# A softmax with temperature on one core: all transfers on one queue in a fixed order, in pieces of 6 MB, with the row maximum subtracted

## The chip, the cores and the metric

The kernel runs on one core of a Trainium2 chip. The metric is the device time of one execution in microseconds (us), lower is better.

## The reference

```python
x = randn(32, 512, 1024).astype(float32); temperature = 0.5
scaled = x / temperature
shifted = scaled - max(scaled, axis=-1, keepdims=True)
exp_x = exp(shifted)
return exp_x / sum(exp_x, axis=-1, keepdims=True)
```

That is 16,384 rows of 1,024 numbers: 67.1 MB read and 67.1 MB written, with about one exponential and one multiplication for each number. In both kernels these 134.2 MB pass through the DMA engines of the core.

## The kernel before

Four rows for each of 128 partitions make a tile of 2 MB. Loads are issued on SP, stores on ACT (two queues), and a pool of eight buffers with automatic waits keeps them running side by side. The kernel doesn't subtract the maximum; with this data (normal numbers times two) the exponential doesn't overflow.

```python
K_MAIN = 4
SPLIT_LAST = 4
# ... sched = 32 tiles of K = 4
data = ctx.enter_context(tc.tile_pool(name="data", bufs=8))
for it, (g0, K) in enumerate(sched):
    # ... xv, ov: rows (p k) of this tile, 16 KB in one piece per partition
    xtile = data.tile([P, K, d], mybir.dt.float32)
    nc.sync.dma_start(out=xtile.rearrange("p k d -> p (k d)"), in_=xv)          # L47
    for j in range(K):
        nc.scalar.activation(xtile[:, j, :], xtile[:, j, :], Exp,               # L52
                             scale=scale, accum_out=sums[:, j : j + 1])
    nc.vector.reciprocal(recip, sums)                                           # L59
    for j in range(K):
        nc.vector.tensor_scalar_mul(xtile[:, j, :], in0=xtile[:, j, :],         # L61
                                    scalar1=recip[:, j : j + 1])
    if it >= ntiles - SPLIT_LAST and K > 1:
        h = K // 2
        nc.scalar.dma_start(out=ov[:, :h, :], in_=xtile[:, :h, :])
        nc.sync.dma_start(out=ov[:, h:, :], in_=xtile[:, h:, :])
    else:
        nc.scalar.dma_start(out=ov, in_=xtile)                                  # L70
```

Of the kernel before, what the change touches and what calls it, by code (L numbers as in the profile page):

```python
# [1 line left out]

# [4 lines left out]


@with_exitstack  # L10
def kernel(
    ctx: ExitStack,
    tc: tile.TileContext,
    x: bass.AP,
    temperature: bass.AP,
    out: bass.AP,
):
    nc = tc.nc
    scale = 1.0 / float(temperature)

    P = 128
    xf = x.flatten_outer_dims()
    of = out.flatten_outer_dims()
    n, d = xf.shape
    nrowgroups = n // P

    K_MAIN = 4
    SPLIT_LAST = 4
    sched = []
    g = 0  # L30
    while g < nrowgroups:
        k = min(K_MAIN, nrowgroups - g)
        sched.append((g, k))
        g += k
    ntiles = len(sched)

    data = ctx.enter_context(tc.tile_pool(name="data", bufs=8))
    stats = ctx.enter_context(tc.tile_pool(name="stats", bufs=16))

    for it, (g0, K) in enumerate(sched):  # L40
        rows = P * K
        r0 = g0 * P
        xv = xf[r0 : r0 + rows, :].rearrange("(p k) d -> p (k d)", p=P, k=K)
        ov = of[r0 : r0 + rows, :].rearrange("(p k) d -> p k d", p=P, k=K)

        xtile = data.tile([P, K, d], mybir.dt.float32)
        nc.sync.dma_start(out=xtile.rearrange("p k d -> p (k d)"), in_=xv)  # L47

        sums = stats.tile([P, K], mybir.dt.float32)
        recip = stats.tile([P, K], mybir.dt.float32)  # L50
        for j in range(K):
            nc.scalar.activation(  # L52
                xtile[:, j, :],
                xtile[:, j, :],
                mybir.ActivationFunctionType.Exp,
                scale=scale,
                accum_out=sums[:, j : j + 1],
            )
        nc.vector.reciprocal(recip, sums)  # L59
        for j in range(K):  # L60
            nc.vector.tensor_scalar_mul(  # L61
                xtile[:, j, :], in0=xtile[:, j, :], scalar1=recip[:, j : j + 1]
            )

        if it >= ntiles - SPLIT_LAST and K > 1:
            h = K // 2
            nc.scalar.dma_start(out=ov[:, :h, :], in_=xtile[:, :h, :])  # L67
            nc.sync.dma_start(out=ov[:, h:, :], in_=xtile[:, h:, :])
        else:
            nc.scalar.dma_start(out=ov, in_=xtile)  # L70


# [1 line left out]
_INS = ['x', 'temperature']  # L74
_OUTS = [((32, 512, 1024), 'float32')]
#: Inputs that are plain numbers.
_NUMBERS = {'temperature': 0.5}


# [26 lines left out]
```

## Time and profile before

| | before |
|---|---|
| time, median | 319.7 us (319.55 to 319.85, 3 runs) |
| span of the profiled execution | 317.8 us |
| DVE / ACT busy | 29% / 43% |
| moved | 134.26 MB, 422 GB/s over the span |

The page's first two parts for the kernel before. The rows of 40 digits divide the span into slices of 7.9 us; a digit is the busy share in tenths, and 9 means 90% or more.

```profile
span 317.8 us, 636 instructions
...
DVE 93.4 (29%) x160; ACT 138.0 (43%) x257; POOL 0.2 (0%) x4
...
DVE  0352333312300517631333213333123003733300
ACT  1875334554321739655334553345543106852500
DMA  7999999999999999999999999999999999999996
GB/s 297 429 394 429 431 431 434 435 433 433 433 429 429 432 429 429 429 429 431 429 433 434 433 435 431 429 433 431 431 429 429 431 429 431 437 429 430 422 426 271
```

DVE and ACT are mostly idle. DMA is full in every slice but the first and the last, at about 430 GB/s. Below are the two queues (packets, MB, share of the 16 DMA engines' time) and the chain that ended last, by engine: the two queues share the same engines half and half, and 91% of the chain is DMA.

```profile
q1 hardware_dynamic: 5184, 71.31, 52.9%
q10 hardware_dynamic: 4608, 62.92, 46.3%
...
DMA 91%; ACT 1%; SPq 1%; DVE 1%; issue 0%; DVEq 0%; ACTq 0%
```

The costliest groups (busy us, mean ns of one, idle time before them), and the transfers (KB each, median us from issue to landing):

```profile
L52 ACT ACTIVATE xtile<-xtile 128x1024 f32<-128x1024 f32 x128 | 133.5, 1044 | 159.3 <-DMA xtile<-in_x_dram 158.2
L61 DVE TENSOR_SCALAR xtile<-xtile,recip 128x1024 f32<-128x1024 f32 x128 | 87.7, 749 | 1.1
...
xtile<-in_x_dram SPq DMA_DIRECT2D x32, 2048.0 KB, 31.3
out_dram<-xtile ACTq DMA_DIRECT2D x28, 2048.0 KB, 24.2
```

Every activation and every multiplication is short against the time that DMA takes for the tile: load and store of 2 MB each are 9.8 us of DMA, against 4 x 1.04 us of ACT and 4 x 0.75 us of DVE.

The last stretches of 2 us (start:end of the stretch, its length, busy time of DVE, ACT and POOL with counts, PEclk, DMA share, GB/s). A packet's bytes are booked where it starts, so a share can exceed 1 and the last rows run a little ahead of the true ends.

```profile
312.00:314.00 2.00, 0.00 (x0) 0.00 (x0) 0.00 (x0) 1.00 1.00 422
314.00:316.00 2.00, 0.00 (x0) 0.00 (x0) 0.00 (x0) 1.00 0.46 193
316.00:318.00 2.00, 0.00 (x0) 0.00 (x0) 0.00 (x0) 1.00 0.01 4
```

The DMA engines run out of work between 314 and 316 us, and the span closes at 317.8.

The page gives the mean of 16 DMA engines.

- *Ends of single engines.* The trace holds a record of each DMA packet (start, duration, size, queue). On a busy engine a packet starts within some 4 ns of the end of the one before, so the records fall into 16 chains, one per engine, by matching ends and starts. A few chains swap partners where two engines happen to run in step, so single chains are approximate; the 16 end times are not affected.
- *Lag of a transfer.* Each transfer is spread over the 16 engines, and each engine adds one completion write to the transfer's semaphore when its share has landed. (The Trainium skill says so in "DMA: Bandwidth & Descriptors", section "Why a DMA increments its semaphore by 16 and not by 1"; the trace agrees: 68 transfers here, and 1,088 packets under 512 B on the queues.)

### The profile page before, as it was taken

Reading aid. Unit: us, or ns where it says so; the run is one execution under the profiler, and the core shown is the slowest. Engines: PE = TensorE matmul, PEld = TensorE weight load, DVE = VectorE, ACT = ScalarE, POOL = GpSimd, SP = SyncE. Lnnn points to the kernel's source line nnn. Section 1 sums busy time; section 2 is a strip of 40 time slices with the busy share of each in tenths; the row PEclk is TensorE's granted clock in tenths of the full one; section 3 lists DMA queues with packets and bytes.
Section 4 is the critical chain, followed back from the end, with each engine's and each line's share of the span. In section 5 each row is a group of like instructions: output and inputs, shape, how many; then the busy total and the mean of one; then the engine's idle time right before and its main releaser. Section 6 shows DMA issues by size and latency. Waiting matters only on the chain.

```text
span 317.8 us, 636 instructions
## 1 busy us (share of the span) xinstructions
DVE 93.4 (29%) x160; ACT 138.0 (43%) x257; POOL 0.2 (0%) x4
## 2 busy tenths in 40 slices
DVE  0352333312300517631333213333123003733300
ACT  1875334554321739655334553345543106852500
POOL 0000000000000000000000000000000000000000
DMA  7999999999999999999999999999999999999996
GB/s 297 429 394 429 431 431 434 435 433 433 433 429 429 432 429 429 429 429 431 429 433 434 433 435 431 429 433 431 431 429 429 431 429 431 437 429 430 422 426 271
DMA packets 9797, 134.26 MB, mean 422 GB/s; under 512 B 1088, under 2 KB 1088, under 8 KB 1088
## 3 DMA queue, kind: packets, MB, share of 16 engines
q1 hardware_dynamic: 5184, 71.31, 52.9%
q10 hardware_dynamic: 4608, 62.92, 46.3%
q14 instruction: 5, 0.04, 0.0%
HBM read 67.11 MB, written 67.11 MB: 422 GB/s over the span
## 4 chain that ended last, share of the span: by engine, by line
DMA 91%; ACT 1%; SPq 1%; DVE 1%; issue 0%; DVEq 0%; ACTq 0%
DMA xtile<-in_x_dram 55%; DMA out_dram<-xtile 36%; ACT xtile L52 1%; SPq L47 1%; DVE xtile L61 1%; DVEq L101 0%; ACTq L67 0%; DVE recip L59 0%; ACTq L52 0%; ACTq L70 0%
## 5 line engine op out<-in xcount | busy, mean ns | idle before, releaser
L52 ACT ACTIVATE xtile<-xtile 128x1024 f32<-128x1024 f32 x128 | 133.5, 1044 | 159.3 <-DMA xtile<-in_x_dram 158.2
L61 DVE TENSOR_SCALAR xtile<-xtile,recip 128x1024 f32<-128x1024 f32 x128 | 87.7, 749 | 1.1
L59 DVE RECIPROCAL recip<-sums 128x4 f32<-128x4 f32 x32 | 5.7, 178 | 206.5 <-ACT xtile L52 206.5
L52 ACT ACTIVATION_READ_ACCUMULATOR xtile<-xtile 128x1 f32 x128 | 23.8, 186 | 0.0
L52 ACT ACT_TABLE_LOAD x1 | 1.3, 1283 | 0.7 <-PEq L87 0.7
L87 POOL MEMSET const-bfloat16-1.0<- 128x1 bf16 x1 | 0.1, 101 | 0.0
L87 POOL MEMSET const-uint8-127<- 128x1 uint8 x1 | 0.1, 101 | 0.0
L87 POOL MEMSET const-float32-0.0<- 128x1 f32 x1 | 0.1, 98 | 0.2 <-issue 0.2
L87 POOL MEMSET const-float32-1.0<- 128x1 f32 x1 | 0.1, 98 | 0.0
## 6 DMA issues: line engine op xcount, KB each, us to landing
xtile<-in_x_dram SPq DMA_DIRECT2D x32, 2048.0 KB, 31.3
out_dram<-xtile ACTq DMA_DIRECT2D x28, 2048.0 KB, 24.2
out_dram<-xtile ACTq DMA_DIRECT2D x4, 1024.0 KB, 22.7
out_dram<-xtile SPq DMA_DIRECT2D x4, 1024.0 KB, 14.9
```

Of the source, the lines that this page charges most:

```text
L47: nc.sync.dma_start(out=xtile.rearrange("p k d -> p (k d)"), in_=xv)
L52: nc.scalar.activation(xtile[:, j, :], xtile[:, j, :], mybir.ActivationFunctionType.Exp, scale=scale, accum_out=sums[:, j : j + 1],)
L59: nc.vector.reciprocal(recip, sums)
L61: nc.vector.tensor_scalar_mul(xtile[:, j, :], in0=xtile[:, j, :], scalar1=recip[:, j : j + 1])
L87: nc = _bacc.Bacc("TRN2", target_bir_lowering=False, num_devices=1)
```

## The change

The intent: one queue (SP) that carries all transfers in a fixed order with a semaphore each, so that nothing depends on a scheduler; larger transfers, since DMA is the limit (22 transfers of 4 to 6 MB instead of 68 of 1 to 2 MB; 48 KB in one piece per partition); a ring of four 48 KB slots per partition in place of eight 16 KB tiles; and the row maximum subtracted as the reference does, computed on DVE, with groups of four rows pipelined over DVE and ACT. The diff, cut to its core:

```diff
-    K_MAIN = 4
-    data = ctx.enter_context(tc.tile_pool(name="data", bufs=8))
+LOADS = [12] * 10 + [8]
+STORES = [[12]] * 10 + [[8]]
+RING = 48
+GROUP = 4
+AHEAD = 1
+    ring = pool.tile([P, RING, d], f32, name="ring")
     # ... places, groups, one semaphore per load and per store
+    def maximum(g):                                    # DVE, L113
+        # ... at the first group of a chunk: wait for loaded[i]
+        nc.vector.tensor_reduce(out=top[:, r : r + k], in_=ring[:, s : s + k, :],
+                                axis=X, op=max).then_inc(topped, 1)
+    def shift(g):                                      # DVE: bias = -scale * top
+    def exponential(g):                                # ACT, L131
+        nc.scalar.wait_ge(biased, g + 1)
+        # ... activation(Exp, bias=bias[:, row], scale=scale, accum_out=sums[:, row])
+    def invert(g): ...                                 # DVE
+    def divide(g): ...                                 # DVE, L150
+    for kind, i, after in _queue(LOADS, STORES, places, AHEAD):   # SP
+        if kind == "load":
+            # ... wait for the stores that free the slot
+            nc.sync.dma_start(out=ring[...], in_=dram(xf, ...)).then_inc(loaded[i], 16)
+        else:
+            nc.sync.wait_ge(scaled, part_end[i])
+            nc.sync.dma_start(out=dram(of, ...), in_=ring[...]).then_inc(stored[i], 16)
+    for g in range(len(groups)):
+        exponential(g)
+    for g in range(len(groups) + 1):                   # DVE
+        if g < len(groups):
+            maximum(g); shift(g)
+        if g > 0:
+            invert(g - 1); divide(g - 1)
```

The order on the queue is L0 L1 L2 L3 S0 S1 L4 S2 L5 S3 L6 S4 L7 S5 L8 S6 L9 S7 L10 S8 S9 S10 (L a load, S a store).

More of the change, by code (lines that the diff above doesn't have):

```diff
@@ L7, with _places, _queue @@
 from concourse._compat import with_exitstack
+LOADS = [12] * 10 + [8]
[3 more added lines that the diff above has]
+AHEAD = 1
+def _places(loads, ring):
+    places, p = [], 0
+    for k in loads:
+        if p + k > ring:
+            p = 0
+        places.append(p)
+        p += k
+    return places
+def _queue(loads, stores, places, ahead):
+    flat = [(i, n) for i, ks in enumerate(stores) for n in range(len(ks))]
+    last = {i: n for n, (i, _) in enumerate(flat)}
+    order, given = [], 0
+    for i, k in enumerate(loads):
+        over = [
+            b
+            for b in range(i)
+            if places[b] < places[i] + k and places[i] < places[b] + loads[b]
+        ]
+        after = max((last[b] for b in over), default=-1)
+        while given <= after + ahead and after >= 0 and flat[given][0] < i:
+            order.append(("store", given, None))
+            given += 1
+        order.append(("load", i, after))
+    order += [("store", n, None) for n in range(given, len(flat))]
+    return order
 @with_exitstack
@@ L18 @@
     nc = tc.nc
+    f32 = mybir.dt.float32
     scale = 1.0 / float(temperature)
+    extreme = mybir.AluOpType.max if scale > 0 else mybir.AluOpType.min
     P = 128
@@ L24 @@
     n, d = xf.shape
-    nrowgroups = n // P
-    K_MAIN = 4
-    SPLIT_LAST = 4
-    sched = []
-    g = 0
-    while g < nrowgroups:
-        k = min(K_MAIN, nrowgroups - g)
-        sched.append((g, k))
-        g += k
-    ntiles = len(sched)
-    data = ctx.enter_context(tc.tile_pool(name="data", bufs=8))
-    stats = ctx.enter_context(tc.tile_pool(name="stats", bufs=16))
-    for it, (g0, K) in enumerate(sched):
-        rows = P * K
-        r0 = g0 * P
-        xv = xf[r0 : r0 + rows, :].rearrange("(p k) d -> p (k d)", p=P, k=K)
-        ov = of[r0 : r0 + rows, :].rearrange("(p k) d -> p k d", p=P, k=K)
-        xtile = data.tile([P, K, d], mybir.dt.float32)
-        nc.sync.dma_start(out=xtile.rearrange("p k d -> p (k d)"), in_=xv)
-        sums = stats.tile([P, K], mybir.dt.float32)
-        recip = stats.tile([P, K], mybir.dt.float32)
-        for j in range(K):
-            nc.scalar.activation(
-                xtile[:, j, :],
-                xtile[:, j, :],
+    assert sum(LOADS) * P == n
@@ new lines @@
+    places = _places(LOADS, RING)
+    first = [sum(LOADS[:i]) for i in range(len(LOADS))]
+    total = sum(LOADS)
+    pool = ctx.enter_context(tc.tile_pool(name="data", bufs=1))
+    ring = pool.tile([P, RING, d], f32, name="ring")
+    top = pool.tile([P, total], f32, name="top")
+    bias = pool.tile([P, total], f32, name="bias")
+    sums = pool.tile([P, total], f32, name="sums")
+    recip = pool.tile([P, total], f32, name="recip")
+    parts = []
+    for i, ks in enumerate(STORES):
+        j = 0
+        for k in ks:
+            parts.append((i, places[i] + j, first[i] + j, k))
+            j += k
+        assert j == LOADS[i]
@@ new lines @@
+    groups, part_end = [], []
+    for i, s, r, k in parts:
+        for a in range(0, k, GROUP):
+            groups.append((i, s + a, r + a, min(GROUP, k - a)))
+        part_end.append(len(groups))
+    loaded = [tc.alloc_semaphore(f"loaded{i}") for i in range(len(LOADS))]
+    stored = [tc.alloc_semaphore(f"stored{i}") for i in range(len(parts))]
+    topped, biased, summed, inverted, scaled = (
+        tc.alloc_semaphore(name)
+        for name in ("topped", "biased", "summed", "inverted", "scaled")
+    )
@@ new lines, in dram @@
+    def dram(t, r, k, i):
+        block = t[P * first[i] : P * (first[i] + LOADS[i]), :]
+        block = block.rearrange("(p k) d -> p k d", p=P, k=LOADS[i])
+        return block[:, r - first[i] : r - first[i] + k, :]
+    def maximum(g):
+        i, s, r, k = groups[g]
+        if g == 0 or groups[g - 1][0] != i:
+            nc.vector.wait_ge(loaded[i], 16)
+        nc.vector.tensor_reduce(
+            out=top[:, r : r + k],
+            in_=ring[:, s : s + k, :],
+            axis=mybir.AxisListType.X,
+            op=extreme,
+        ).then_inc(topped, 1)
@@ L55 @@
+    def shift(g):
+        i, s, r, k = groups[g]
+        nc.vector.wait_ge(topped, g + 1)
+        nc.vector.tensor_scalar_mul(
+            bias[:, r : r + k], in0=top[:, r : r + k], scalar1=-scale
+        ).then_inc(biased, 1)
+    def exponential(g):
+        i, s, r, k = groups[g]
+        nc.scalar.wait_ge(biased, g + 1)
+        for a in range(k):
+            ins = nc.scalar.activation(
+                ring[:, s + a, :],
+                ring[:, s + a, :],
                 mybir.ActivationFunctionType.Exp,
+                bias=bias[:, r + a : r + a + 1],
@@ L56 @@
                 scale=scale,
-                accum_out=sums[:, j : j + 1],
+                accum_out=sums[:, r + a : r + a + 1],
             )
-        nc.vector.reciprocal(recip, sums)
-        for j in range(K):
-            nc.vector.tensor_scalar_mul(
-                xtile[:, j, :], in0=xtile[:, j, :], scalar1=recip[:, j : j + 1]
-            )
-        if it >= ntiles - SPLIT_LAST and K > 1:
-            h = K // 2
-            nc.scalar.dma_start(out=ov[:, :h, :], in_=xtile[:, :h, :])
-            nc.sync.dma_start(out=ov[:, h:, :], in_=xtile[:, h:, :])
-        else:
-            nc.scalar.dma_start(out=ov, in_=xtile)
+        ins.then_inc(summed, 1)
@@ new lines, in invert, with divide @@
+    def invert(g):
+        i, s, r, k = groups[g]
+        nc.vector.wait_ge(summed, g + 1)
+        nc.vector.reciprocal(recip[:, r : r + k], sums[:, r : r + k]).then_inc(inverted, 1)
+    def divide(g):
+        i, s, r, k = groups[g]
+        nc.vector.wait_ge(inverted, g + 1)
+        for a in range(k):
+            ins = nc.vector.tensor_scalar_mul(
+                ring[:, s + a, :], in0=ring[:, s + a, :], scalar1=recip[:, r + a : r + a + 1]
+            )
+        ins.then_inc(scaled, 1)
@@ new lines @@
+    done_to = -1
+    with tc.tile_critical():
+        for kind, i, after in _queue(LOADS, STORES, places, AHEAD):
+            if kind == "load":
+                for b in range(after + 1):
+                    if b > done_to:
+                        nc.sync.wait_ge(stored[b], 16)
+                done_to = max(done_to, after)
+                s, r, k = places[i], first[i], LOADS[i]
+                nc.sync.dma_start(
+                    out=ring[:, s : s + k, :], in_=dram(xf, r, k, i)
+                ).then_inc(loaded[i], 16)
+            else:
+                l, s, r, k = parts[i]
+                nc.sync.wait_ge(scaled, part_end[i])
+                nc.sync.dma_start(
+                    out=dram(of, r, k, l), in_=ring[:, s : s + k, :]
+                ).then_inc(stored[i], 16)
+        for b in range(len(parts)):
+            if b > done_to:
+                nc.sync.wait_ge(stored[b], 16)
+        for g in range(len(groups)):
+            exponential(g)
+        for g in range(len(groups) + 1):
+            if g < len(groups):
+                maximum(g)
+                shift(g)
+            if g > 0:
+                invert(g - 1)
+                divide(g - 1)
```

## The prediction

> **What bounds the kernel now.** DMA, from end to end. The page's first two parts show DVE busy 29% and ACT 43% of the 317.8 us span, but the DMA row reads 9 in every slice except the first (7) and last (6), at about 430 GB/s. The chain that ended last is 91% DMA. Both directions share the same engines: the load-only start (430 GB/s per slice) runs no faster or slower than the mixed middle (431), and all 134.2 MB at that rate are already 312 us. The timing windows put everything else at the ends: data starts about 1.8 us into the span, flows at full rate until about 312, and the last bytes and their receipt end at 317.8. The runs' time (319.7) is 1.9 us above the span. The Trainium skill, "DMA: Bandwidth & Descriptors", section "Where 436 GB/s comes from", gives a ceiling of 435.2 GB/s; this trace holds 99% of it, so an estimated floor is 134.2/435.2 = 308.4 us plus 5 us of ends: about 313.5. Two per cent would be 313.3. It is out of reach unless the ends shrink.
>
> **What the change does.**
> - Queue: everything on SP in a fixed order. I expect nothing from this: the load-only start, which is one queue, runs at full rate.
> - Transfer size: 68 transfers of 1 to 2 MB become 22 of 4 to 6 MB, and a packet grows from 16 KB to 48 KB. In the packet records of the trace a 16 KB packet follows the one before on its engine after 607 ns, an 8 KB one after 306, so about 301 ns per 8 KB plus 5 fixed. Per engine before: 480 x 607 + 64 x 306 = 311.0 us. After, estimated: 160 x 1811 + 16 x 1209 = 309.1. Gain 1.9 us, all of it on the critical path; fewer completion writes give perhaps 0.3 more.
> - DVE: 32 row-maximum reductions over 128x4096, at one element a cycle (skill, "VectorE: DVE Perf Modes", tier table) estimated at 4.4 us each, plus 32 tiny scalings. DVE busy rises from 93 to about 238 us (75%). ACT stays at about 138.
> - Slack: I walked the queue. A 6 MB transfer takes 14.6 us. A chunk takes DVE about 23.5 us against 29 us of DMA per load and store. First store needed at 60 us, ready at 40; second needed at 75, ready at about 69 (tightest, since DVE starts only when 6 MB have landed, near 17.5); third needed at 104, ready at 93. Later each store is ready 15 us or more early, though a chunk's last division waits behind the next chunk's first maximum. At the end the last-but-one store has about 5 us of slack. So the added vector work is hidden.
> - Ends: the same start latency and the same receipt.
>
> **Prediction.** 319.7 - 2.2 = 317.5 us, range 315.6 to 319.8. Faster by over 2%: 0.03; within 2%: 0.93; slower by over 2%: 0.04.
>
> **What would show it.** Packets of 48 KB lasting about 1.81 us; DMA slices of 9 throughout at 432 to 435 GB/s; SP waiting on stores and divisions while DMA stays full; reductions near 4.4 us; DVE near 238 us; chain still over 90% DMA.
>
> **What would make it wrong.** Packets split again to 16 KB or less (no gain: about 319.5). The second store late, if reductions or their semaphore waits cost over 1 us more per group: a hole of a few us near 75 us. One queue leaving a gap where loads turn to stores. A larger spread between engines at the end, as pieces are bigger.

## More of the kernel before

The median of 16 values is here the eighth or the mean of the eighth and ninth; the two differ by some 0.1 us or less. In the kernel before, the first packet starts 1.76 us into the span, the median engine ends at 314.85 and the last at 316.5.

Where a semaphore belongs to one transfer alone, as in the changed kernel, the last of its 16 completion times minus their median says how far the slowest engine is behind.

## The result, and the profile after

| | before | after |
|---|---|---|
| time, median | 319.77 us (319.55 to 319.86, 4 runs) | 321.02 us (320.71 to 321.83, 4 runs) |
| ratio after/before | | 1.0045, 95% interval 1.0031 to 1.0059 |
| span of the profiled execution | 317.8 us | 320.0 us |
| DVE / ACT busy | 29% / 43% | 73% / 47% |

A ratio here and below is the mean time of one kernel's fast runs over that of the kernel before in the same rounds, so it isn't quite the ratio of the medians. The change costs 0.45%. That is within the 2% which the prediction gave 0.93, but 1.2 us above the end of its range; 317.5 was predicted.

The same parts of the page, for the kernel after:

```profile
span 320.0 us, 557 instructions
...
DVE 235.1 (73%) x224; ACT 149.7 (47%) x257; POOL 0.2 (0%) x4
...
DVE  0069999999999699389909964993799199798300
ACT  1009665555666355526615650565166246646000
DMA  7999999999999999999999999999999999999992
GB/s 295 473 405 455 430 399 479 394 400 455 430 405 467 399 461 412 412 473 399 473 399 436 436 412 473 406 448 424 399 473 406 461 412 424 444 424 418 444 424 98
```

```profile
q1 hardware_dynamic: 3168, 134.22, 97.8%
...
DMA 74%; DVE 16%; ACT 3%; issue 0%; SPq 0%
```

```profile
L131 ACT ACTIVATE ring<-ring,bias 128x1024 f32<-128x1024 f32 x128 | 145.5, 1137 | 146.0 <-DVE bias L123 146.0
L113 DVE TENSOR_REDUCE top<-ring 128x4 f32<-128x4096 f32 x32 | 141.3, 4415 | 60.2 <-DMA ring<-in_x_dram 60.2
L150 DVE TENSOR_SCALAR ring<-ring,recip 128x1024 f32<-128x1024 f32 x128 | 87.7, 749 | 1.1
...
ring<-in_x_dram SPq DMA_DIRECT2D x10, 6144.0 KB, 44.3
out_dram<-ring SPq DMA_DIRECT2D x10, 6144.0 KB, 34.2
```

What was predicted of the engines came: DVE is at 235.1 us (predicted 238), a reduction takes 4.415 us (predicted 4.4, from the rate that the Trainium skill gives in the tier table of "VectorE: DVE Perf Modes": 4,096 elements at one a cycle), and DMA is full in every slice but the ends. An activation takes 95 ns longer with the bias operand (1,137 ns against 1,042 in the run no_max below); the Trainium skill, "ScalarE: Activation LUTs", section "What ACT_TABLE_LOAD costs", gives about 93 ns for each per-partition operand. None of it matters for the time (no_max shows that below). One thing expected of the page did not come: the chain is 74% DMA and not over 90%, as it now runs through the maximum and the division in front of some stores. The DMA engines were full meanwhile, so this cost nothing. The one queue waited for data only where it was meant to, while transfers issued earlier kept the DMA engines busy (SP's waits: line, waited for, us in total, times, longest):

```profile
SPq L171 <- DVE ring L150: 245.4, 11, 43.1
SPq L165 <- DMA out_dram<-ring: 45.1, 7, 9.7
SPq L176 <- DMA out_dram<-ring: 18.6, 2, 9.6
```

L171 is a store that waits for its division, L165 a load that waits for a slot, L176 the end. DMA had work all the while.

The difference is at the end. The last stretches of the kernel after, to be read against those of before:

```profile
312.00:314.00 2.00, 0.00 (x0) 0.00 (x0) 0.00 (x0) 1.00 0.53 229
314.00:316.00 2.00, 0.00 (x0) 0.00 (x0) 0.00 (x0) 1.00 0.27 115
316.00:318.00 2.00, 0.00 (x0) 0.00 (x0) 0.00 (x0) 1.00 0.11 49
```

The mean engine is done *earlier* than before (0.53 of the DMA time used from 312 to 314 us, where before used all of it), but some engine still moves data from 316 to 318 us. By the single engines' ends:

| us into the span | before | after | difference |
|---|---|---|---|
| first packet | 1.76 | 1.95 | +0.19 |
| median engine ends | 314.85 | 313.43 | |
| ... from the first packet | 313.09 | 311.48 | -1.61 |
| last engine ends | 316.51 | 318.29 | |
| ... behind the median one | 1.66 | 4.86 | +3.20 |
| span ends | 317.82 | 320.04 | |
| ... after the last completion write, which lands 0.33 us behind the last engine's end in both | 0.98 | 1.42 | +0.44 |

The sum of the differences is 0.2 - 1.6 + 3.2 + 0.4 = 2.2 us, which is that of the two spans. (The profiled execution of the kernel after was its slowest of four, 0.8 us above their median. An ordinary run may have that much less of lag; only this one was profiled.) The gain from longer packets is there on most engines; four are 2.6 to 4.9 us behind, and the kernel waits for the last. And the lateness grows through the whole run. The lag of each transfer, in the order of the queue (us):

```
L0 1.3  L1 1.3  L2 1.3  L3 1.7   S0 1.7  S1 1.3  L4 2.6   S2 2.4  L5 2.7   S3 2.4
L6 3.4   S4 3.2  L7 3.5   S5 3.4  L8 4.4   S6 4.2  L9 4.6   S7 4.6  L10 4.8   S8 4.9  S9 4.9  S10 4.8
```

It goes up at loads that a store follows, and not at the stores. The steps are uneven: 1.0 to 1.3 us at L4, L6 and L8, and 0.4 or less at the others. A figure "per turn" below is an average over the turns of one profiled execution. The packet records show the same in detail. A 48 KB packet takes 1,815 ns, nearly always. At the first turn (L3 to S0) every engine's last load packets together take about 0.8 us longer. At the later turns only the engines that are already behind lose time, in their last load packets: from L4 to S2 the three latest engines lost 1.1, 0.7 and 0.4 us and the other thirteen 0.1 us each on average; from L8 to S6 the four latest lost 1.0, 1.0, 0.9 and 0.7 us and the others nothing. Summed over all engines and the turns after the first, loads in front of a store lost 15 us of engine time, stores in front of a load 0.3 us.

The theories at this point:

1. *Turns.* On one queue each engine does a run of loads, then a store, then loads. An engine that is behind is still loading when the others store, its last load packets are held up then, and it falls further behind. Two queues have loads and stores on every engine all the time, so there are no such turns.
2. *Size.* 48 KB packets or 6 MB transfers as such make the engines uneven.
3. *Added work.* The row maximum, which keeps DVE busy for 73% of the time and reads all data once more, disturbs the transfers.

### The profile page after: what moved, and what is told of

Same layout as the page of the kernel before. It is cut to its first block, busy times and chain, and to the rows that moved or that the text cites. A ratio compares the mean times of both kernels' runs of the same rounds, so it can differ in the third digit from the quotient of the medians.

```text
span 320.0 us, 557 instructions
## 1 busy us (share of the span) xinstructions
DVE 235.1 (73%) x224; ACT 149.7 (47%) x257; POOL 0.2 (0%) x4
## 4 chain that ended last, share of the span: by engine, by line
DMA 74%; DVE 16%; ACT 3%; issue 0%; SPq 0%
DMA ring<-in_x_dram 41%; DMA out_dram<-ring 33%; DVE top L113 10%; DVE ring L150 6%; ACT ring L131 3%; DVE bias L123 0%; DVE recip L144 0%; SPq L219 0%; SPq L156 0%
## 5 line engine op out<-in xcount | busy, mean ns | idle before, releaser
L131 ACT ACTIVATE ring<-ring,bias 128x1024 f32<-128x1024 f32 x128 | 145.5, 1137 | 146.0 <-DVE bias L123 146.0
L113 DVE TENSOR_REDUCE top<-ring 128x4 f32<-128x4096 f32 x32 | 141.3, 4415 | 60.2 <-DMA ring<-in_x_dram 60.2
L150 DVE TENSOR_SCALAR ring<-ring,recip 128x1024 f32<-128x1024 f32 x128 | 87.7, 749 | 1.1
L131 ACT ACTIVATION_READ_ACCUMULATOR ring<-ring,bias 128x1 f32 x128 | 23.9, 187 | 0.0
L123 DVE TENSOR_SCALAR bias<-top 128x4 f32<-128x4 f32 x32 | 5.4, 170 | 1.1
```

Source lines behind the costliest of these rows:

```text
L113: nc.vector.tensor_reduce(out=top[:, r : r + k], in_=ring[:, s : s + k, :], axis=mybir.AxisListType.X, op=extreme,).then_inc(topped, 1)
L123: nc.vector.tensor_scalar_mul(bias[:, r : r + k], in0=top[:, r : r + k], scalar1=-scale).then_inc(biased, 1)
L131: ins = nc.scalar.activation(ring[:, s + a, :], ring[:, s + a, :], mybir.ActivationFunctionType.Exp, bias=bias[:, r + a : r + a + 1], scal ...
L150: ins = nc.vector.tensor_scalar_mul(ring[:, s + a, :], in0=ring[:, s + a, :], scalar1=recip[:, r + a : r + a + 1])
```

## The experiments

All 14 kernels gave correct results. "Last behind median" is the end of the last DMA engine minus that of the median one in the profiled execution. The kernel before had medians of 319.6 to 319.8 us in all rounds.

| kernel | queues | MB, packet | maximum | time us | ratio to before (95%) | last behind median us |
|---|---|---|---|---|---|---|
| before | 2 | 2, 16 KB | no | 319.7 | | 1.7 |
| after | 1 | 6, 48 KB | yes | 321.0 | 1.0045 (1.0031-1.0059) | 4.9 |
| two_queues | 2 | 6, 48 KB | yes | 321.5 | 1.0060 (1.0046-1.0073) | 0.1 (hole, see text) |
| runs_16k | 1 | 6, 16 KB | yes | 321.6 | 1.0059 (1.0046-1.0071) | 3.2 |
| no_max | 1 | 6, 48 KB | no | 321.1 | 1.0036 (1.0022-1.0049) | 3.9 |
| small_2mb | 1 | 2, 16 KB | yes | 322.9 | 1.0098 (1.0085-1.0112) | 3.8 |
| two_queues_fix | 2 | 6, 48 KB | yes | 323.8 | 1.0150 (1.0119-1.0180) | 5.1 |
| small_2mb_two_queues | 2 | 2, 16 KB | yes | 320.0 | 1.0011 (0.9999-1.0023) | 1.4 |
| pairs | 1 | 6, 48 KB | yes | 320.0 | 1.0013 (1.0001-1.0025) | 2.9 |
| before_4mb | 2 | 4, 32 KB | no | 318.0 | 0.9947 (0.9935-0.9959) | 1.0 |
| one_queue_4mb | 1 | 4, 32 KB | yes | 322.0 | 1.0073 (1.0059-1.0087) | 5.3 |
| two_queues_4mb | 2 | 4, 32 KB | yes | 324.0 | 1.0139 (1.0126-1.0153) | 2.1 (all late) |
| before_6mb | 2 | 6, 48 KB | no | **317.2** | 0.9930 (0.9917-0.9942) | 0.9 |
| two_queues_no_max | 2 | 6, 48 KB | no | 318.3 | 0.9960 (0.9947-0.9974) | 1.1 |
| two_queues_short_max | 2 | 6, 48 KB | a quarter | 318.8 | 0.9969 (0.9956-0.9983) | 1.7 |
| triples_no_max | 1 | 6, 48 KB | no | 319.8 | 1.0003 (0.9991-1.0016) | 1.7 (hole, see text) |

### two_queues

```diff
-            else:                                   # SP
-                nc.sync.wait_ge(scaled, part_end[i])
-                nc.sync.dma_start(out=dram(of, r, k, l), in_=ring[:, s : s + k, :]) ...
+        for g in range(len(groups) + 2):            # ACT
+            if g < len(groups): exponential(g)
+            if g - 1 in part_end: store(part_end.index(g - 1))   # nc.scalar: wait, dma_start
```

> The changed kernel with its stores issued on ACT instead of SP; same 6 MB transfers, same waits. Theory 1 (turnaround: in one queue the last load packet in front of a store is held up 0.5 to 1 us on some engines, it adds up on unlucky engines, and the end waits for the slowest): two queues hide it, 317.3 to 318.5 us, last engine within 2 us of the median one (after: 5 us). Theory 2 (size: 48 KB packets and 6 MB transfers make the engines uneven): stays at 320.5 to 321.5. Theory 3 (the added vector work disturbs the transfers): stays at 320.5 to 321.5.

Measured: 321.5 us, which looks like theories 2 and 3. The profile says otherwise: there is a hole (DMA share and GB/s are the last two columns).

```profile
284.00:288.00 4.00, 3.93 (x8) 2.99 (x5) 0.00 (x0) 1.00 0.94 406
288.00:292.00 4.00, 4.00 (x1) 1.65 (x4) 0.00 (x0) 1.00 0.09 37
292.00:296.00 4.00, 3.14 (x7) 3.61 (x7) 0.00 (x0) 1.00 0.92 393
```

The engines ended within 0.2 us of each other, but only because all of them stood idle together near 290 us and started again together. The last store but one was ready at 288 us and was issued at 292.4: it stood on ACT behind an exponential that itself waited for the next maximum. The fault was in the experiment, and it decides nothing about the time. Two things can be kept. Up to the last load the lag of the transfers stayed between 0.6 and 1.7 us, apart from one value of 2.2, and without the 4 us of hole the kernel would have been near 317.5 (an estimate: 321.5 less the hole). The second attempt, two_queues_fix below, did not bear that estimate out.

### runs_16k

```diff
-        block = block.rearrange("(p k) d -> p k d", p=P, k=LOADS[i])
-        return block[:, r - first[i] : r - first[i] + k, :]
+        return block.rearrange("(c p k) d -> p c (k d)", p=P, k=4)   # three 16 KB pieces per partition
```

> The changed kernel with every 6 MB transfer cut into 16 KB runs (packets of 16 KB instead of 48 KB), same transfers and queue. Theory 1: the hold-ups stay and the packet overhead of 1.9 us comes back, 321.5 to 323.5 us. Theory 2: engines even again, 319 to 320. Theory 3: 322 to 323.

Measured: 321.6 us. The median engine ends at 314.8, as before the change: the packet gain is gone. The last is still 3.2 us behind it. Theory 2 had expected small packets to make the engines even again, and they don't, although the lag is smaller than with long ones.

### no_max

```diff
-        nc.scalar.wait_ge(biased, g + 1)
+        if g == 0 or groups[g - 1][0] != i: nc.scalar.wait_ge(loaded[i], 16)
-                bias=bias[:, r + a : r + a + 1],
-            maximum(g); shift(g)
```

> The changed kernel without the row maximum (exponential of the plain scaled value, as before); queue and transfers the same. Theories 1 and 2: 320.5 to 321.5 us, unchanged, with DVE busy back near 93 us. Theory 3: 317.5 to 318.5, the hold-ups gone.

Measured: 321.1 us with DVE busy 93.4 us again, and a lag that grows from 0.9 us to 3.9. In the changed kernel the row maximum costs no time, and theory 3 falls for it.

### small_2mb

```diff
-LOADS = [12] * 10 + [8]
-STORES = [[12]] * 10 + [[8]]
+LOADS = [4] * 32
+STORES = [[4]] * 32
```

> The changed kernel with 32 transfers of 2 MB each way, still one queue in fixed order: about 21 alternations of load and store instead of 8. Theory 1: more hold-ups, 322.5 to 327 us. Theory 2: 319 to 320, as in the kernel before. Theory 3: 322 to 323.

Measured: 322.9 us, with the size of the kernel before and one queue. The lag grows from 0.5 to 3.8 us. So the sizes of the kernel before don't help. Theory 1's time came, but not wholly for its reason: 21 turns gave no more lag than eight turns with 48 KB packets did (0.16 us per turn against 0.44). Another 0.8 us comes after the end of the transfers: from the last completion write to the end of the span it takes 2.2 us, against 1.4 in the changed kernel and 1.0 before. The instruction there that clears the semaphores takes 0.44 us, 0.20 and 0.09, with 69, 27 and no semaphores of the kernel's own.

### two_queues_fix

```diff
         for g in range(len(groups) + 1):            # DVE
+            edge = g == len(groups) or g == 0 or groups[g][0] != groups[g - 1][0]
+            if g > 0 and edge: invert(g - 1); divide(g - 1)
             if g < len(groups): maximum(g); shift(g)
-            if g > 0: invert(g - 1); divide(g - 1)
+            if g > 0 and not edge: invert(g - 1); divide(g - 1)
+        for g in range(len(groups) + 1):            # ACT
+            if g in part_end: store(part_end.index(g))
+            if g < len(groups): exponential(g)
```

> Two queues again (stores on ACT), with the hole of the first attempt taken away: each chunk's last division goes before the next chunk's first maximum, and its store is issued right behind it. Theory 1 (one queue lets engines that lag be held up at each turn from load to store): no hole, engines end within 2 us of each other, 316.3 to 318.2 us, 3 to 5 us under the changed kernel. Theory 2 (large packets and transfers as such make engines uneven): last engine still 4 us behind the median, 319.5 to 321.

Measured: 323.8 us, and the runs scatter from 322.8 to 326.6. This contradicted theory 1 as I had put it: two queues alone are not enough. In the packet records the harm is done between 42 and 75 us, when stores have begun and loads aren't over. Ten engines do load and store packets in turn at 1,815 ns each; the other six, which made one load packet more before their first store and so do the opposite of the ten, have store packets of about 2,440 ns again and again, and the stores of this stretch lag by up to 7.7 us. The runs two_queues_no_max and two_queues_short_max below show that the row maximum brings it about, though not how.

### small_2mb_two_queues

The kernel small_2mb with its stores on ACT, each issued behind the exponentials of the next group.

```diff
+        for g in range(len(groups) + 1):            # ACT
+            if g > 0 and g - 1 in part_end: store(part_end.index(g - 1))
+            if g < len(groups): exponential(g)
+        store(len(parts) - 1)
```

> The 2 MB one-queue kernel (322.9 us) with its stores on ACT. Theory 1: the lag of single engines goes from 3.8 us to under 2, 319.5 to 321 us (the end still carries the clearing of many semaphores). Theory 2: 322 to 323.5, no change from the queue.

Measured: 320.0 us against 322.9 with one queue. Transfers, semaphores, arithmetic and maximum are the same; only the queue of the stores and the moment of their issue differ. The last engine is 1.4 us behind instead of 3.8. Of the 2.9 us between the two profiled spans, 2.4 are the earlier end of the last engine; 0.5 fall after the last completion write (1.7 us against 2.2), and the turns don't explain those.

### pairs

```diff
+    plan = "L0 L1 L2 L3 S0 S1 L4 L5 S2 S3 L6 L7 S4 S5 L8 L9 S6 S7 L10 S8 S9 S10"
```

> The changed kernel, one queue, but two stores and two loads in turn: 5 turns from load to store instead of 8, everything else the same. Theory 1: fewer hold-ups, 318.8 to 320.6 us, last engine 2 to 4 us behind the median. Theory 2: 320.5 to 321.5, unchanged.

Measured: 320.0 us, 1.0 below the changed kernel. The lag grows from 0.7 us to 2.9 over five turns, against 1.3 to 4.8 over eight: 0.44 us per turn in both. Only the order of the transfers on the one queue was changed.

### before_4mb

```diff
-    K_MAIN = 4
-    data = ctx.enter_context(tc.tile_pool(name="data", bufs=8))
+    K_MAIN = 8
+    data = ctx.enter_context(tc.tile_pool(name="data", bufs=6))
```

> The kernel before with tiles of 4 MB and six buffers (packets of 32 KB), two queues as it has them. Theory 1: the packet gain of about 1.5 us arrives since two queues keep the engines even: 317.3 to 319 us. Theory 2: engines uneven, 319.5 to 321.

Measured: 318.0 us, as theory 1 expected. Two constants of the old kernel, with its two queues and automatic waits left alone, bring most of the gain that the change was predicted to bring.

### one_queue_4mb and two_queues_4mb

```diff
-LOADS = [12] * 10 + [8]
+LOADS = [8] * 15 + [4, 4]
-STORES = [[12]] * 10 + [[8]]
+STORES = [[8]] * 15 + [[4], [4]]
```

once in the changed kernel and once in two_queues_fix.

> The changed kernel with 4 MB transfers (packets of 32 KB, ring of six slots), one queue, about 10 turns from load to store. Theory 1 (in one queue an engine that lags is held up when the others turn to storing): last engine 3 to 5 us behind the median, 320.5 to 322.5 us. Theory 2 (only the 48 KB packets make the engines uneven): even engines, 318 to 319.5.

> Its twin with the stores on ACT, row maximum kept; a chunk's last division ahead of the next chunk's first maximum. Theory 1: even engines, 317.8 to 319.3 us, that is the enlarged kernel before (318.0) plus about 0.6 for the later start and the clearing of semaphores. Theory 2: the same time as its twin within 0.7 us.

Measured: 322.0 and 324.0 us. The first is theory 1's: lag from 0.5 us to 5.3 over 11 turns, 0.44 us per turn, with 32 KB packets. The second missed both theories. Its last engine isn't far behind, but all are late (median end 317.9 us): on every engine 6 to 14 of the some 83 load packets in front of a store are held up by 0.1 to 0.8 us, and on ten engines there is a hole of 0.3 to 2 us near 312 us, before the last store. It shares the row maximum and the order of issue with two_queues_fix. What the two have in common was tried next.

### before_6mb

```diff
-    K_MAIN = 4
-    SPLIT_LAST = 4
-    data = ctx.enter_context(tc.tile_pool(name="data", bufs=8))
+    K_MAIN = 12
+    SPLIT_LAST = 0
+    data = ctx.enter_context(tc.tile_pool(name="data", bufs=4))
```

> The kernel before with 6 MB tiles and four buffers, two queues, packets of 48 KB. What is open since the second attempt at two queues with 6 MB came out uneven: if 48 KB packets are uneven in two queues too, last engine 3 to 5 us behind and 320 to 323 us; if that was particular to that kernel, 317.5 to 319.5.

Measured: 317.2 us, the best of all, 0.7% under the kernel before. This settles theory 2: 48 KB packets in 6 MB transfers on two queues have the last engine 0.9 us behind. The page's parts 1 to 3 of before_6mb (span, DMA share and GB/s by slice, queues):

```profile
span 315.5 us, 489 instructions
...
DMA  8999999999999999999999999999999999999996
GB/s 324 461 411 436 449 344 467 399 449 449 399 480 418 399 480 418 400 486 411 411 480 405 424 467 405 442 444 411 449 436 411 467 422 426 418 470 418 411 442 283
...
q1 hardware_dynamic: 1584, 67.11, 49.8%
q10 hardware_dynamic: 1584, 67.11, 49.1%
```

DMA is full in every slice, as in the slow kernels; this row doesn't tell them apart. From the first stores on, each engine does load and store packets in turn, and a load packet in front of a store loses 1 ns on average (in the kernel after 136 ns, the 15 us above over seven turns and 16 engines). So changing direction isn't costly in itself: on two queues an engine does it at nearly every packet. In the kernel after, the losses fall on the engines that still load while the others store.

### two_queues_no_max

The kernel no_max with its stores on ACT, by the edit of small_2mb_two_queues.

> The one-queue kernel without the row maximum (321.1 us) with its stores issued on ACT: the cleanest pair for the queue, same 6 MB transfers, ring, semaphores and arithmetic. Theory 1 (one queue is the cause): 317.4 to 318.4 us, last engine within 2 us of the median, near the enlarged kernel before (317.2) plus about 0.6. If the manual ring and its waits are the cause instead: 320.5 to 324. And against the two-queue kernel with the maximum (323.8): if the late stores of the maximum are what spoiled that one, it goes down to 318 here.

Measured: 318.3 us against 321.1, a difference of 2.8 us. The two ran in different rounds; by their ratios to the kernel before it is 2.4 us. This is the cleanest pair: the same 6 MB transfers, ring, semaphores and arithmetic; the stores are on the other queue and go out as soon as they are ready. The lag no longer grows: once stores have begun it stays between 2.3 and 2.6 us for the loads and 1.1 and 1.4 for the stores, to the end. The last stretches of no_max (one queue):

```profile
312.00:314.00 2.00, 0.00 (x0) 0.00 (x0) 0.00 (x0) 1.00 0.69 295
314.00:316.00 2.00, 0.00 (x0) 0.00 (x0) 0.00 (x0) 1.00 0.23 98
316.00:318.00 2.00, 0.00 (x0) 0.00 (x0) 0.00 (x0) 1.00 0.04 16
```

and of two_queues_no_max:

```profile
312.00:314.00 2.00, 0.00 (x0) 0.00 (x0) 0.00 (x0) 1.00 0.65 279
314.00:316.00 2.00, 0.00 (x0) 0.00 (x0) 0.00 (x0) 1.00 0.00 0
316.00:318.00 2.00, 0.00 (x0) 0.00 (x0) 0.00 (x0) 1.00 0.00 0
```

From 312 to 314 us both do nearly the same amount of work, so their mean engines end together (median ends 313.7 and 313.6). After 314 no packet starts any more with two queues, and the last engine ends at 314.7 us; with one queue it ends at 317.6. The manual ring and its waits are cleared too.

### two_queues_short_max

```diff
-            in_=ring[:, s : s + k, :],
+            in_=ring[:, s : s + k, : d // 4],
```

The maximum of a quarter of the row is no true maximum; the softmax is the same for any shift that doesn't overflow.

> The second attempt at two queues (323.8 us) with the maximum taken over the first quarter of each row only (any shift gives the same softmax for this data): same instructions, same order, about 3.3 us less DVE time per group. If the late stores behind a busy DVE are what spoiled that kernel, 317.8 to 319 us, as without the maximum (318.3). If it is the order of issue itself, 322 to 324.

Measured: 318.8 us against 323.8. The span and DVE's busy time of two_queues_fix:

```profile
span 321.1 us, 557 instructions
...
DVE 236.9 (74%) x224; ACT 148.5 (46%) x257; POOL 0.2 (0%) x4
```

and of two_queues_short_max:

```profile
span 317.3 us, 557 instructions
...
DVE 135.8 (43%) x224; ACT 147.4 (46%) x257; POOL 0.2 (0%) x4
```

Instructions, order and issue are the same, and only the reduction is shorter. So on two queues with this order the row maximum does cost about 5 us, though on the one queue it costs nothing. A shorter reduction takes less time and also reads less; the run doesn't separate the two. That it acts through stores that come late and put the engines out of step is my reading of the packet records, and no run shows it.

### triples_no_max

```diff
+    plan = "L0 L1 L2 L3 S0 S1 S2 L4 L5 L6 S3 S4 S5 L7 L8 L9 S6 S7 S8 L10 S9 S10"
```

> The one-queue kernel without the maximum (321.1 us, 8 turns from load to store) with three stores and three loads in turn: 4 turns. If the loss grows with the turns that single engines make late, 319 to 320.4 us; if it comes from having one queue in some other way, 320.7 to 321.5.

Measured: 319.8 us, inside what theory 1 gave, but the run isn't clean. With only one other store (S9) between L10 and its own store, that last store wasn't ready in time:

```profile
302.00:304.00 2.00, 2.00 (x4) 0.00 (x0) 0.00 (x0) 1.00 0.40 172
304.00:306.00 2.00, 0.61 (x1) 0.00 (x0) 0.00 (x0) 1.00 0.63 270
```

Most engines stood idle for about 2 us and the late ones caught up meanwhile. Up to there the lag had grown from 1.5 us to 3.7 over four turns, 0.55 us per turn, against 0.37 over eight in no_max. It ended nearly as high (3.7 against 3.9), as it started higher. I count this run as inconclusive; that fewer turns cost less rests on pairs.

## Why the prediction was wrong

The prediction was 317.5 us (315.6 to 319.8), and the kernel took 321.0. Point by point:

- *"What bounds the kernel now. DMA, from end to end."* Right. DMA stayed full in every kernel.
- *The packet gain of 1.9 us.* Right in mechanism and nearly in size: 48 KB packets follow each other every 1,812 ns (1,811 was estimated), and the median engine needs 1.6 us less. runs_16k takes it away again.
- *Vector work and slack.* Right for this kernel: DVE was busy 235.1 us, the first store issued at 46 us (needed at 60), second at 68 (needed at 75), third at 91 (needed at 104). Taking the maximum out doesn't change the time (321.1).
- *"I expect nothing from this: the load-only start, which is one queue, runs at full rate."* **This is the step that failed.** The load-only start has no turn from loading to storing, so it could not show what turns cost on one queue. On one queue the slowest DMA engine falls behind at these turns, by 0.37 to 0.44 us per turn on average with packets of 32 and 48 KB, and in the end it is 3 to 5 us late. Fewer turns in the changed kernel itself (pairs) took its lag from 4.9 to 2.9 us and its time down by 1.0. Putting the stores on the other queue gave 2.8 us (6 MB without the maximum) and 2.9 us (2 MB with it). But with the full maximum and long transfers two queues were no gain: 321.5 and 323.8 us against 321.0 (6 MB), and 324.0 against 322.0 (4 MB). The packet records show other losses there.
- *"Per engine before: ... After, estimated: ... Gain 1.9 us, all of it on the critical path."* That sum was for an average engine. The time is set by the last one. A mean over 16 engines, the DMA row of the page included, can't show this.
- *"One queue leaving a gap where loads turn to stores"* stood among the things that would make the prediction wrong. The place was right. There was no gap, since DMA stayed full; the packets of the late engines took longer.
- *"A larger spread between engines at the end, as pieces are bigger"* stood there too. The spread was it, the reason was not: before_6mb has the same pieces and 0.9 us of spread, small_2mb has the old pieces and 3.8.
- *"Ends: the same start latency and the same receipt."* A small miss: 0.2 us later start and 0.4 us more at the close, part of it the clearing of 27 semaphores. Between two_queues_no_max and before_6mb (spans of 316.5 and 315.5 us) the same two places make 0.7 us of the 1.0, though their orders of issue differ as well.

What stays open. Why a late engine's last load packets are held up while the others store isn't known; the records show that and on which engines it happens. The lag per turn wasn't the same for all sizes (0.16 us with 2 MB), and the triples run, which would have tested it again, wasn't clean. Each lag was read from one profiled execution. And on two queues with the full row maximum three kernels with long packets were slow (321.5 with its hole, 323.8 and 324.0) and one with short ones was not (320.0). The maximum is part of the cause there, and the rest was not found. A kernel with the full maximum that beats the kernel before was not found either; before_6mb, which beats both, leaves the maximum out as the kernel before does.

## What to carry to other kernels

Where DMA is the limit, look at the end of each DMA engine and at the spread of each transfer's completion writes, not only at the mean share: a full DMA row can hide engines that are 5 us late. Try loads and stores on two queues, and measure it: here two queues gained 2.8 and 2.9 us in two pairs of kernels and lost 2 to 3 in two others, which had the full row maximum and long transfers. Where one queue must do, try fewer turns between loading and storing: the one clean test of that here gained 1.0 us. Before one reorganises a kernel to get longer transfers, it is worth trying three constants of the old one: here that was worth 0.7%, and the reorganisation -0.45%.

## What the Trainium skill lacked or had wrong

- "DMA: Bandwidth & Descriptors", section "Issuing engines are not separate DMA queues", says that starting DMAs from several engines "will only save the time on the sequencer it takes to initiate the DMA", and the rules at the page's end say that spreading them doesn't help bandwidth. The rate of the median engine indeed stayed the same (ends at 313.7 and 313.6 us), but "only" is too strong: the second queue was worth 2.8 us of 321.1 with the same transfers (two_queues_no_max against no_max), and 2.9 us of 322.9 (small_2mb_two_queues against small_2mb). Issue took about 0.34 us per transfer in either kernel of the first pair and was hidden behind a full queue. With the full maximum and 4 or 6 MB transfers the second queue was no gain.
- The same page says that the engines of one transfer finish independently, but not that their lag can grow from transfer to transfer, nor what a turn from loading to storing costs on one queue: in these runs the lag of the slowest grew by 0.37 to 0.44 us per turn with 32 and 48 KB packets, up to 5.3 us (one_queue_4mb), and by 0.16 with 16 KB packets (small_2mb).
- The same page has rates by transfer size and a fixed overhead per packet for small descriptors, but no time for packets of 16 KB and more: here 16 KB packets followed each other every 607 ns and 48 KB packets every 1,812 ns, 9 ns less than three of the former, and the median engine of 134 MB ended 1.6 us earlier.
- No page has the cost of clearing semaphores inside the kernel's own span; "Runtime: NRT & Kernel Launch" has only the runtime's reset around a kernel. Here the clearing instruction took 0.09 us with no semaphores of the kernel's own, 0.20 with 27 and 0.44 with 69.
